# Transposes of a constant in TensorE's expected gaps, and up weights requested at the top of a step, in a hybrid mixer and feed-forward layer

## The chip, the cores and the metric

The kernel runs on one core of a Trainium2 chip. The metric is the device time of one execution in microseconds (us). The engines are TensorE (PE, with its weight loads PEld), VectorE (DVE), ScalarE (ACT), GpSimd (POOL) and SyncE (SP), which issues every DMA in this kernel.

## The reference

One layer over a sequence of 2048 tokens of width 1024, float32 throughout:

```python
def reference(x, norm1_w, w_in, ...):
    for l in range(DEPTH):                       # DEPTH = 1
        h = rms_norm(x, norm1_w[l])
        proj = h @ w_in[l]                       # 1024 -> 3344 columns
        (g_q, g_k, g_v, g_z, g_b, g_a, m_q, m_k, m_v, m_o, m_i, m_f, s_u) = jnp.split(proj, split_idx, axis=-1)
        y_a = gated_deltanet(g_q, g_k, g_v, g_z, g_b, g_a, ...)   # 4 heads of 128, conv of 4 taps, chunked delta rule
        y_b = mlstm(m_q, m_k, m_v, m_o, m_i, m_f, ...)            # 4 heads of 64, chunked
        y_c = s5_mixer(s_u, ...)                                  # 16 groups of 16 channels, 64 complex states
        y = jnp.concatenate([y_a, y_b, y_c], axis=-1)
        x = x + y @ w_out[l]
        x = x + conv_ffn(rms_norm(x, norm2_w[l]), w_up[l], ffn_conv_w[l], ffn_conv_b[l], w_down[l])
    return rms_norm(x, final_norm_w)

def conv_ffn(x, w_up, conv_w, conv_b, w_down):   # D_FF = 2816
    h = causal_depthwise_conv(x @ w_up, conv_w) + conv_b          # 3 taps
    gate, up = jnp.split(h, 2, axis=-1)
    return (jax.nn.silu(gate) * up) @ w_down
```

## The kernel before

Large products are done as three matmuls of a type fp32r: each operand is split into a rounded high part (an ACT copy) and a low part (a subtraction, mostly on POOL), and high x high, high x low and low x high are summed in PSUM (`split`, `mm`).

*Mixing stage (`main_a`).* The sequence is cut in 4 blocks of 512 tokens. For each block some 26 projections of 128 columns (`proj`, 24 matmuls of 512 columns each) run in an order written out in `ORDER`. Each is followed by `follow`, which drains its PSUM bank and starts the convolution, and when a head's value projection is through, a generator `gdn` for that head. `gdn` computes the chunked delta rule of one head and one block: transposes, Gram products, an inverse in six levels, and then a chain over 4 chunks in which three matmuls alternate with DVE and ACT reads of the same PSUM tile `sq0` or `sq1` (by the parity of n = 4 x block + head; three quarters of the tile are used). `mlstm`, `gates` and the `s5_` functions are further generators. The last two projections of a block run interleaved in `last_two`, while the next block's normed input is transposed. `w_split` splits the projection weights ahead; `w_two` lowers the number it may keep ready.

*Who goes next.* The whole program is laid out by a planner at build time; each engine executes its own instructions in exactly that order, and waits at run time only on semaphores. `Engine` wraps an engine: each call is first entered into a `Clock`, then emitted. `Clock.note` computes when the instruction could start (the engine free, its inputs written, PSUM readers taking turns, outputs free) and how long it takes by fixed costs: a transpose of n columns 2n/2400 us (0.107 us for 128), an fp32r matmul n/2400 + 0.0025. A PSUM tile counts as one piece there. The loop `drive` asks the running generators in turn, and steps the one whose needs are met earliest by that clock. When nothing is ready the clock moves on: there it expects TensorE to stand.

*Output product.* `out_proj` multiplies the mixed output by `w_out`; when the mixers are through, `ffn_pools` closes the PSUM pool of the mixing stage and opens that of the feed-forward stage.

*Feed-forward stage (`ffn`).* Two halves of 1024 tokens. For each, 22 pairs of an up product by `up_pair`, which multiplies the 2 x 2 blocks with 7 products instead of 8 (operand sums of the weights made by POOL in `sum12` and `make`), then two down products of 512 tokens (`down`), whose result is normed and stored by `final`. Weights come through a ring: `raw_load` issues a DMA of 512 KB into one of NRAW = 4 raw tiles `f_wr`; `make` takes the next item of `todo` (kinds U, M, D), splits it into parts `f_ph`, `f_pl` (NPART = 8), and marks raw tiles free in `freed`. The next call of `make` issues the loads for these. `make` is called after every product (`up_pair`) or block of products (`down`). It returns at once when the ring has no free slot, or when the next item is of kind U and the up stage's pool `fu` is not open:

```python
        if not self.todo or self.ring < (1 if self.todo[0][0] == "U" else 2):
            return
        G = self.G
        kind, j = self.todo[0]
        if kind == "U" and self.fu is None:
            return

        while self.freed:
            self.freed -= 1
            self.raw_load()
```

Names in the profile: psq, psz, psx and the like are PSUM banks of projections and transposes, sd_ names those of `gdn`, sq its chain, psf the up and psd the down product, f_S the sums of raw weights, d_x and d_h, d_l the down product's moving blocks. Nearly all instructions have the line of the wrapper `call` (L169).

Of the kernel before, what the change touches and what calls it, by code (L numbers as in the profile page):

```python
# [7 lines left out]
F32 = mybir.dt.float32  # L8
# [9 lines left out]
P = 128  # L18
# [5 lines left out]
NCB = BT // P  # L24
# [22 lines left out]
class Clock:  # L47
# [5 lines left out]
    def __init__(self):  # L53
        self.free = {e: 0.0 for e in ("T", "V", "A", "G", "S", "dge", "dma")}
        self.wr, self.rd, self.table, self.slots = {}, {}, None, {}
        self.cold = 0.0
# [46 lines left out]
                t = max(t, end + own.get(by, other))  # L103
        return t

    def note(self, e, op, args, kw):
        out = kw.get("out", args[0] if args else None)
        outs = [self.span(a) for a in (out, kw.get("accum_out")) if a is not None]
        ins = [v for k, v in kw.items() if k not in ("out", "accum_out") and hasattr(v, "tensor")]

        turns = [self.span(v) for v in ins if v.space == PSUM]
        ins = [self.span(v) for v in ins]
        t = self.free[e]
        for a in ins:
            t = max(t, self.after(self.wr, a, {e: self.DRAIN[e]}, self.SEM))
        for a in turns:
            t = max(t, self.after(self.rd, a, {e: -1.0}, self.SEM))
        for a in outs:
            for log in (self.wr, self.rd):
                t = max(t, self.after(log, a, {e: -1.0}, self.SEM))  # L120
        if e == "S":
            self.free["S"] = t + 0.05
            self.free["dge"] = max(self.free["dge"], t) + 0.46
            n = out.shape[0] * self.size(out) * 4
            self.free["dma"] = max(self.free["dma"], self.free["dge"]) + n / 360e3
            end = self.free["dma"] + 1.6
        else:
            c = self.cost(e, op, out, kw)
            if e == "T":
                c += min(c, max(0.0, self.cold - t))  # L130
            end = self.free[e] = t + c
        for name, rs in ins:
            d = self.rd.setdefault(name, {})
            if end > d.get(rs, (0.0, e))[0]:
                d[rs] = (end, e)
        for name, rs in outs:
            for log in (self.wr, self.rd):
                d = log.setdefault(name, {})
                for k in [k for k in d if all(any(lo <= a and b <= hi for lo, hi in rs) for a, b in k)]:
                    del d[k]  # L140
            self.wr[name][rs] = (end, e)
# [18 lines left out]
class Engine:  # L160
    def __init__(self, clock, key, eng):
        self.clock, self.key, self.eng = clock, key, eng

    def __getattr__(self, op):
        f = getattr(self.eng, op)

        def call(*args, **kw):
            self.clock.note(self.key, op, args, kw)
            return f(*args, **kw)  # L169
        return call  # L170
# [18 lines left out]
class Hybrid:  # L189
# [32 lines left out]
    def exp(self, y, x, n, r, q, i):  # L222
# [9 lines left out]
        V.tensor_scalar(out=i, in0=n, scalar1=127.0, scalar2=8388608.0, op0=ALU.add, op1=ALU.mult)  # L232
        V.scalar_tensor_tensor(out=y, in0=q, scalar=1.0, in1=i.bitcast(F32), op0=ALU.add, op1=ALU.mult)


    def setup(self):
        nc, ins, V, A, S = self.nc, self.ins, self.V, self.A, self.S
        cp = self.const = self.pool("const")
        self.dram = self.pool("dram", space=DRAM)
        self.pctx = ExitStack()  # L240
        self.ps = self.pool("ps", space=PSUM, ctx=self.pctx)
        self.ident = cp.tile([P, P], F32, name="ident")
        S.dma_start(out=self.ident, in_=self.cst_d[C_ID])

# [258 lines left out]
    def last_two(self, b, n, ops, take, follow):  # L503

        pr = []
        self.kdone = 0
        for j, (kind, i) in enumerate(ops):
            w, ps = yield from take(kind, i, n + j)
            pr.append((kind, i, ps, self.proj(ps, *w)))
            self.w_two = j  # L510
            if j == 0:
                self.add_side(self.norm_next(b + 1, n + 2), True)
        for k in range(KD):
            for p in pr:
                yield next(p[3])
            self.kdone = k + 1
        self.w_two = 0
        for kind, i, ps, g in pr:
            for _ in g:
                pass  # L520
            follow(kind, i, ps)
# [106 lines left out]
    def main_a(self):  # L628
        self.posts = self.posted = self.drained = self.hblock = n = 0
        for b in range(NB):  # L630
            st = {"tiles": [[] for _ in range(H)], "z": [[] for _ in range(H)]}

            def take(kind, i, n):
                if kind == "q":
                    yield lambda: len(self.gdn_live) < 4
                if kind in "qz":
                    yield lambda: self.y_done > b * H + i - (Q_BUFS if kind == "q" else Z_BUFS)
                if kind == "mq" and i == 0:
                    yield lambda: not self.ml_busy
                    self.ml_busy = True  # L640
                    for nm in ("mk", "mv", "mo"):
                        st[nm] = self.mp.tile([P, 2, BT], F32, tag=nm, name=nm)
                yield lambda: self.w_rdy
                w = self.w_rdy.pop(0)
                if n == 0:
                    yield lambda: self.xdone >= b
                    yield tuple(self.xq)
                if b and kind == "g":
                    yield lambda: len(self.hN[1]) > 4
                tag = f"b{n % 3}"  # L650
                yield w[1], tag, lambda: self.drained >= n - 2
                return w, self.ps.tile([P, BT], F32, tag=tag, bufs=1, name="ps" + kind)

            def follow(kind, i, ps):
                self.add_side(self.post(self.follow(b, kind, i, ps, st)))
                if kind == "v":
                    self.gdn_live.append(Side(self.gdn(b, i, st["tiles"][i], st["z"][i], st)))

            ops = [op[:2] for op in self.ops_a(b)]
            last = ops[-2:] if b < NB - 1 else []  # L660
            for kind, i in ops[:len(ops) - len(last)]:
                w, ps = yield from take(kind, i, n)
                if kind == "g":
                    yield from self.norm1(n, ps, w) if b == 0 else self.proj_next(ps, *w)
                else:
                    yield from self.proj(ps, *w)
                n += 1
                follow(kind, i, ps)
            if last:
                yield from self.last_two(b, n, last, take, follow)  # L670
                n += 2
# [94 lines left out]
    def gdn(self, b, h, tiles, gz, gt):  # L766
        V, A, G, T, S = self.V, self.A, self.G, self.T, self.S
        n = b * H + h
# [3 lines left out]
        sh = [P, NCB, P]  # L772
# [34 lines left out]
        kdec = big("kdec", 3)  # L807
# [18 lines left out]
        rs, t = sm("rs", 2 * NCB), sm("t", 2 * NCB)  # L826
        self.rsqrt(rs, ssq, t)
        rk, rq = rs[:, 0:NCB], rs[:, NCB:2 * NCB]
        c1, b2, nc2 = sm("c1"), sm("b2"), sm("nc2")
# [26 lines left out]
        vb = c3(vT)  # L856
# [10 lines left out]
        for lev in range(1, NM):  # L867
# [6 lines left out]
            for c in range(NCB):  # L874
# [4 lines left out]
                            op=ALU.mult)  # L879
# [23 lines left out]
        self.inv_done += 1  # L903
        yield Vi

        tag = f"sq{n % 2}"
        yield lambda: self.seq_done[n % 2] == n // 2
        states = [self.Sst[h]]
        yield vb, kdec, states[0], tag
        p = self.ps.tile(sh, F32, tag=tag, bufs=1, name=tag)  # L910
        for c in range(NCB):
            T.matmul(out=p[:, 0, :], lhsT=cs(kT, c), rhs=states[c], start=True, stop=True)
            V.scalar_tensor_tensor(out=vb[:, c, :], in0=p[:, 0, :], scalar=nc2[:, c:c + 1], in1=vb[:, c, :],
# [554 lines left out]
    def ffn_pools(self):  # L1468

        self.wctx.close()  # L1470
        self.lctx.close()
        self.pctx.close()
        self.ps = self.pool("ps2", space=PSUM)
        self.bufs = {"big": 5, "sd": 3, "y": 1, "yh": 2, "yl": 2}
        self.bq = self.operands(self.pool("kp", ctx=self.rctx), 5)
        self.fw = self.pool("fw", ctx=self.rctx)
        self.op = self.pool("op", ctx=self.octx)
        self.ffn_plan()
        self.add_side(self.first_build())
# [209 lines left out]

    def make(self):  # L1690

        if not self.todo or self.ring < (1 if self.todo[0][0] == "U" else 2):
            return
        G = self.G
        kind, j = self.todo[0]
        if kind == "U" and self.fu is None:
            return

        while self.freed:
            self.freed -= 1  # L1700
            self.raw_load()
        self.todo.pop(0)
        if kind != "U":
            w = self.raws.pop(0)
# [315 lines left out]

    def run(self):
        self.now = 0.0
        self.bufs = {"b0": 1, "b1": 1, "b2": 1, "sd": 3, "sq0": 1, "sq1": 1, "e_X": 1, "acc": 3, "wh": 3, "wl": 3,
                     "y": 1, "yh": 2, "yl": 2}
        self.misc, self.gdn_live, self.ml_live = [], [], []
        self.inv_done = self.e_done = self.y_done = 0
# [89 lines left out]
```

## Time and profile before

| | |
|---|---|
| time, median of 3 runs | 2985.22 us (2973.05 to 2985.95) |
| time of the profiled execution | 2976.19 us |
| its span, first to last instruction | 2974.2 us |
| busy, share of the span | PE 91%, PEld 75%, DVE 71%, ACT 44%, POOL 45% |
| mean granted TensorE clock | 0.958 of full speed |
| DMA | 312.69 MB, 105 GB/s over the span |

The page's second part cuts the span in 40 slices of 74 us; each digit is the busy share in tenths, and PEclk is the clock that the throttle granted to TensorE. The mixing stage with the output product takes about the first half of the span, feed-forward the second. In a row of the timeline, the time in brackets is the engine's idle time before the instruction, and after the arrow stands what ended it. A matmul's duration is from its start to its modelled end; the time it takes of the engine is from its start to the next one's start.

### The profile page before, as it was taken

To read this page: it belongs to the slowest core of one execution; us is meant where nothing else is said; L and a number is where in the kernel's file an instruction comes from. 1 tells how busy PE (TensorE), PEld (TensorE's weight loads), DVE (VectorE), ACT (ScalarE), POOL (GpSimd) and SP (SyncE) were. 2 spreads that over 40 slices of the span, in tenths; PEclk is the share of its full clock that TensorE was granted. 3 is DMA by queue.
4 is the path that set the end of the run, shared out by engine and by line. 5 is a ranking of instruction groups with operands and counts; after the bars stand their busy time and mean duration, and the time that the engine had idled before them with its cause. 6 is when DMAs were issued, how large, how long until landed. Compare 5 with 4: busy or idle time off the path is not lost.

```text
span 2974.2 us, 38960 instructions
## 1 busy us (share of the span) xinstructions
PE 2708.9 (91%) x13298; PEld 2234.2 (75%) x13298; DVE 2114.7 (71%) x4346; ACT 1294.9 (44%) x2798; POOL 1325.8 (45%) x960
## 2 busy tenths in 40 slices
PE   6797788988998989889998999999998999999997
PEld 5686677877887778577776888877786888887876
DVE  6876668678765886663558888887546998895364
ACT  4544344444544354632335444445333554543232
POOL 3361122223322243221137888862225998883221
PEclk9898789989999999989999999999999999999999
DMA  4223212133222324335653222235552222224452
GB/s 123 77 84 95 79 46 80 54 90 99 63 59 61 93 77 113 91 97 184 213 175 102 78 86 81 76 107 191 187 181 71 85 86 85 76 81 138 163 177 103
DMA packets 364380, 312.69 MB, mean 105 GB/s; under 512 B 41043, under 2 KB 299222, under 8 KB 364182
## 3 DMA queue, kind: packets, MB, share of 16 engines
q1 hardware_dynamic: 364182, 310.21, 33.4%
q8 instruction: 105, 1.72, 0.2%
q14 instruction: 93, 0.76, 0.1%
HBM read 245.01 MB, written 65.14 MB: 104 GB/s over the span
## 4 chain that ended last, share of the span: by engine, by line
PE 49%; DVE 4%; issue 3%; POOL 1%; ACT 1%; DMA 1%; SPq 0%; DVEq 0%; ACTq 0%; POOLq 0%
PE psf L169 28%; PE psd L169 14%; PE pso L169 4%; POOL f_pl L169 1%; DMA x_d<-o_x 1%; DVE acc L169 0%; PE psx L169 0%; PE sd_pw L169 0%; DVE bl L169 0%; POOL f_S L169 0%; DVE d_l L169 0%; PE pz L169 0%; PE sd_p L169 0%; DVE d_ss L169 0%; PE sq L169 0%
## 5 line engine op out<-in xcount | busy, mean ns | idle before, releaser
L169 POOL TENSOR_TENSOR f_pl<-f_wr,f_ph 128x512 fp32r<-128x512 f32 x274 | 407.5, 1490 | 455.8 <-ACT f_ph L169 425.1
L169 POOL TENSOR_TENSOR wl<-wr,wh 128x1024 fp32r<-128x1024 f32 x108 | 258.5, 2396 | 582.3 <-ACT wh L169 518.9
L169 PE MATMUL psf<-bh,f_pl 128*128 128x512 f32 x1232 | 491.5, 399 | 10.8 <-POOL f_pl L169 10.8
L169 PE MATMUL psf<-bh,f_ph 128*128 128x512 f32 x1232 | 491.7, 399 | 6.3 <-ACT f_ph L169 4.2
L169 PE MATMUL psf<-bl,f_ph 128*128 128x512 f32 x1232 | 491.5, 399 | 1.4 <-DVE bl L169 1.3
L169 DVE SCALAR_TENSOR_TENSOR f_cv<-f_rw,fpar,f_cv 128x512 f32<-128x512 f32 x352 | 480.2, 1384 | 17.5 <-ACT f_rw L169 11.3
L169 ACT ACTIVATE f_ph<-f_wr 128x512 fp32r<-128x512 f32 x360 | 212.4, 619 | 233.9 <-issue 177.0
L169 PEld LDWEIGHTS psf<-bh,f_pl 128*128 128x128 f32 x1232 | 233.8, 190 | 68.9 <-POOL f_pl L169 12.1
L169 PEld LDWEIGHTS psf<-bh,f_ph 128*128 128x128 f32 x1232 | 233.8, 190 | 64.4 <-ACT f_ph L169 5.0
L169 PEld LDWEIGHTS psf<-bl,f_ph 128*128 128x128 f32 x1232 | 233.7, 190 | 60.0 <-DVE bl L169 3.1
L169 ACT ACTIVATE f_cv<-f_rw,fpar 128x512 f32<-128x512 f32 x176 | 142.9, 812 | 307.5 <-DVE f_rw L169 305.1
L169 PE MATMUL psd<-f_ph,d_h 128*128 128x512 f32 x640 | 253.8, 397 | 9.2 <-ACT f_ph L169 8.1
L169 PE MATMUL psd<-f_pl,d_h 128*128 128x512 f32 x640 | 252.7, 395 | 4.9 <-DVE f_pl L169 3.8
L169 PE MATMUL psd<-f_ph,d_l 128*128 128x512 f32 x640 | 252.3, 394 | 1.1 <-DVE d_l L169 1.1
L169 POOL TENSOR_TENSOR f_pl<-f_S,f_ph 128x512 fp32r<-128x512 f32 x132 | 218.7, 1659 | 8.3 <-ACT f_ph L169 4.4
L169 DVE TENSOR_TENSOR f_pl<-f_wr,f_ph 128x512 fp32r<-128x512 f32 x86 | 84.3, 989 | 174.7 <-ACT f_ph L169 174.7
L169 PEld LDWEIGHTS psd<-f_ph,d_h 128*128 128x128 f32 x640 | 121.4, 190 | 36.6 <-ACT f_ph L169 8.7
L169 PEld LDWEIGHTS psd<-f_pl,d_h 128*128 128x128 f32 x640 | 121.4, 190 | 32.9 <-DVE f_pl L169 4.6
L169 PEld LDWEIGHTS psd<-f_ph,d_l 128*128 128x128 f32 x640 | 121.4, 190 | 29.9 <-DVE d_l L169 2.8
L169 ACT ACTIVATE wh<-wr 128x1024 fp32r<-128x1024 f32 x108 | 114.1, 1056 | 39.8 <-PE psz L169 20.8
L169 ACT ACT_TABLE_LOAD x83 | 106.5, 1283 | 31.8 <-DVE acc L169 29.6
L169 POOL TENSOR_TENSOR yl<-y,yh 128x1024 fp32r<-128x1024 f32 x16 | 39.3, 2456 | 167.6 <-ACT yh L169 167.6
(524 smaller groups left out, 6343.7 us busy)
## 6 DMA issues: line engine op xcount, KB each, us to landing
wr<-in_w_in_dram SPq DMA_DIRECT2D x104, 512.0 KB
f_wr<-in_w_up_dram SPq DMA_DIRECT2D x88, 512.0 KB
f_wr<-in_w_down_dram SPq DMA_DIRECT2D x88, 512.0 KB
mid_d<-f_cv SPq DMA_DIRECT2D x88, 256.0 KB
d_x<-mid_d SPq DMA_DIRECT2D x80, 256.0 KB
xt<-in_x_dram SPq DMA_DIRECT2D x16, 512.0 KB
y<-y_d SPq DMA_DIRECT2D x16, 512.0 KB
d_a<-x_d SPq DMA_DIRECT2D x32, 256.0 KB
```

The lines of the kernel that those rows point to most:

```text
L169: return f(*args, **kw)
```

## The change

`Engine` gets a hook `idle`. On TensorE it is set to the new function `spin` from the first `follow` of the mixing stage until `ffn_pools`. Before each TensorE instruction, the wrapper asks the planner's clock when it could start and hands the difference to TensorE's free time to `spin`. If that is over 0.5 us, `spin` emits as many transposes of the 128 x 128 identity as fill 60% of the difference by the planner's cost. They write into the fourth quarter of `sq1`'s bank, which nothing reads. For this, `sq0` and `sq1` become two tiles that are allocated once; a head no longer asks for a tag. In `last_two`, `w_two` is set before the projection's weights are taken, not after. In `make`, the loads for freed raw tiles are issued before the tests for a free slot and an open pool.

```diff
-    def note(self, e, op, args, kw):
+    def begin(self, e, op, args, kw):
...
+        return t, out, outs, ins
+
+    def note(self, e, op, args, kw):
+        t, out, outs, ins = self.begin(e, op, args, kw)
...
 class Engine:
     def __init__(self, clock, key, eng):
         self.clock, self.key, self.eng = clock, key, eng
+        self.idle = None
...
         def call(*args, **kw):
+            if self.idle:
+                self.idle(self.clock.begin(self.key, op, args, kw)[0] - self.clock.free[self.key])
             self.clock.note(self.key, op, args, kw)
...
+    def spin(self, gap):
+
+        if gap > 0.5:
+            self.T.idle = None
+            for _ in range(int(0.6 * gap * 2400 / (2 * P))):
+                self.T.transpose(out=self.spill, in_=self.ident, identity=self.ident)
+            self.T.idle = self.spin
...
+        self.sq = [self.ps.tile([P, NCB, P], F32, name=f"sq{i}") for i in range(2)]
+        self.spill = self.sq[1][:, 3, :]
...
         for j, (kind, i) in enumerate(ops):
+            self.w_two = j
             w, ps = yield from take(kind, i, n + j)
             pr.append((kind, i, ps, self.proj(ps, *w)))
-            self.w_two = j
...
             def follow(kind, i, ps):
+                self.T.idle = self.spin
...
-        tag = f"sq{n % 2}"
         yield lambda: self.seq_done[n % 2] == n // 2
         states = [self.Sst[h]]
-        yield vb, kdec, states[0], tag
-        p = self.ps.tile(sh, F32, tag=tag, bufs=1, name=tag)
+        yield vb, kdec, states[0]
+        p = self.sq[n % 2]
...
         self.lctx.close()
+        self.T.idle = None
         self.pctx.close()
...
     def make(self):
 
+
+        while self.freed:
+            self.freed -= 1
+            self.raw_load()
         if not self.todo or self.ring < (1 if self.todo[0][0] == "U" else 2):
             return
...
-
-        while self.freed:
-            self.freed -= 1
-            self.raw_load()
         self.todo.pop(0)
```

More of the change, by code (lines that the diff above doesn't have):

```diff
@@ L2022, in run @@
         self.now = 0.0
-        self.bufs = {"b0": 1, "b1": 1, "b2": 1, "sd": 3, "sq0": 1, "sq1": 1, "e_X": 1, "acc": 3, "wh": 3, "wl": 3,
+        self.bufs = {"b0": 1, "b1": 1, "b2": 1, "sd": 3, "e_X": 1, "acc": 3, "wh": 3, "wl": 3,
                      "y": 1, "yh": 2, "yl": 2}
```

## The prediction

> **What bounds the kernel now.** I read the page first, for engine shares and the granted clock in 40 slices, then the busy times of chosen stretches, the waits of TensorE and the timeline around its longest stalls.
>
> ```profile
> PE 2708.9 (91%) x13298; PEld 2234.2 (75%) x13298; DVE 2114.7 (71%) x4346; ACT 1294.9 (44%) x2798; POOL 1325.8 (45%) x960
> PE   6797788988998989889998999999998999999997
> PEclk9898789989999999989999999999999999999999
> ```
>
> The same by stretch (columns: length, busy time and count of each engine, granted clock, DMA share, GB/s). The first row is the mixing stage in which the transposes can be emitted, the second the feed-forward stage.
>
> ```profile
> core 0: us, PE busy (x) PEld busy (x) DVE busy (x) ACT busy (x) POOL busy (x), PEclk, DMA share, GB/s
> 29.00:1345.00 1316.00, 1140.61 (x6553) 972.99 (x6552) 935.61 (x2749) 593.09 (x1306) 391.52 (x356) 0.93 0.28 82
> 1600.00:2976.00 1376.00, 1321.34 (x5622) 1063.26 (x5620) 1023.24 (x1213) 589.41 (x1276) 840.95 (x548) 0.98 0.34 113
> 100.00:150.00 50.00, 34.95 (x170) 28.54 (x169) 41.46 (x122) 27.97 (x68) 14.39 (x10) 0.83 0.29 84
> 250.00:300.00 50.00, 32.08 (x190) 28.54 (x189) 22.68 (x78) 25.18 (x63) 7.13 (x3) 0.84 0.33 106
> 300.00:350.00 50.00, 39.12 (x196) 32.82 (x196) 27.23 (x96) 16.37 (x45) 7.30 (x4) 0.79 0.23 74
> 1250.00:1300.00 50.00, 39.32 (x203) 31.02 (x203) 34.86 (x76) 23.79 (x46) 12.79 (x6) 0.80 0.37 118
> ```
>
> Feed-forward is TensorE end to end (1321 of 1376 us). The mixing stage has 1316 - 1141 = 175 us of TensorE idle time and a mean clock of 0.93. The clock is not a smooth quantity; in steps of 3.41 us it is 1.00 or 0.50:
>
> ```profile
> 239.20:242.61 3.41, 1.50 (x14) 1.31 (x15) 3.27 (x12) 0.37 (x1) 0.39 (x1) 1.00 0.54 153
> 242.61:246.02 3.41, 3.41 (x13) 3.02 (x13) 3.20 (x19) 0.64 (x2) 0.00 (x0) 0.50 0.00 1
> 949.15:952.56 3.41, 0.42 (x2) 0.00 (x1) 0.00 (x0) 3.13 (x4) 2.04 (x1) 1.00 0.00 0
> 952.56:959.39 6.83, 4.55 (x21) 4.55 (x22) 3.74 (x9) 5.28 (x8) 0.30 (x1) 0.50 0.38 115
> 962.81:966.22 3.41, 1.97 (x12) 1.25 (x12) 2.79 (x8) 1.68 (x4) 1.64 (x1) 1.00 0.17 41
> 966.23:969.64 3.41, 0.95 (x5) 0.71 (x6) 1.70 (x3) 3.31 (x13) 0.00 (x0) 1.00 0.65 191
> 969.64:973.05 3.41, 3.41 (x12) 2.75 (x12) 2.67 (x7) 0.64 (x3) 0.00 (x0) 0.50 0.00 0
> ```
>
> A step with little work (1.50, 0.42, 0.95 us busy) is followed by one at half speed, in which TensorE has its backlog to do (3.41 of 3.41 busy); a step with 1.97 us busy is followed by full speed. Half-clock time in the mixing stage is 2 x 0.07 x 1316 = 184 us. In the four slices above, rich in it, TensorE is busy 145.5 of 200 us, 73%; so about 134 us of its work runs at half speed, and 67 us of TensorE time is the most that a warm clock returns.
>
> **Change 1: the transposes.** Where the planner's clock expects one TensorE instruction to start more than 0.5 us after TensorE is free, 60% of that gap is filled with transposes of the identity. Do transposes hold the clock, and what does one cost?
>
> ```profile
> 17.34 2.18 PE L169 MATMUL psx<-ident,xt 128*128 128x128 f32 x9 [2.34 <-DVE sg L169]
> 19.17 0.78 PE L169 MATMUL psg<-hh,wh 128*128 128x512 f32 x1
> ...
> 22.96 0.60 PE L169 MATMUL psx<-ident,xt 128*128 128x128 f32 x4
> 23.32 0.48 PE L169 MATMUL psg<-hh,wh 128*128 128x512 f32 x1
> ...
> 963.22 1.97 PE L169 MATMUL psx<-ident,xt 128*128 128x128 f32 x12 [1.77 <-DVE hl L169]
> ```
>
> From start to next start, four took 0.36 us at full clock (0.09 each) and nine took 1.83 us at half clock (0.20 each); the planner books 0.107. The step 962.81 to 966.22 held these twelve transposes and nothing else, 1.97 us, and the next step is still at 1.00: they count. The Trainium skill, "TensorE: Matmul & The Clock Gate", Part 4 (PE-mode transpose), speaks against the change: it says that full speed does not engage for transposes, which do not count as busy in the same way. The row above disagrees.
>
> Gain. Sixty per cent of even an empty step is 2.05 us, above the 1.97 that held the clock; the step at 949.15 would come to 0.42 + 0.6 x 2.99 = 2.21. So a stall that the planner foresees keeps the clock, and what is not foreseen loses it as now. I take 60% foreseen: 40 of the 67 us. What a faster TensorE hands on to the end is bounded by none (the other engines' chain sets the pace) and all. The waits name DVE and ACT:
>
> ```profile
> PE sd_v L169 <- DVE g_D L169: 10.1, 6, 3.9
> PE psx L169 <- DVE hl L169: 10.0, 5, 3.4
> PE sq L169 <- DVE g_kdec L169: 8.3, 6, 3.5
> ```
>
> but DVE is busy only 936 of 1316 us there, TensorE 1141, so I take half: -20 us, ends 0 and -67. Late next is DVE, the releaser of most of these waits.
>
> Cost. If the planner saw exactly the 175 us of idle time, 105 us of transposes (some 1000) would go in, all into time that is empty: 0. If none of it were really empty, TensorE would have 105 us more work. The planner is static and counts no half clock, so some is wrongly placed: I take a fifth, 21 us, half of it handed on, +10 (ends 0 and +105). In a gap that begins at half clock a transpose takes 0.20 us instead of the booked 0.107, and the filling overruns the gap by a fifth; that is in the same term.
>
> The target is the fourth quarter of the second state-chain tile. The planner books a PSUM tile as a whole, so for it a transpose waits for the last DVE or ACT reader of that tile. Whether the program's semaphores do so too, no row shows. If so, before a chain matmul of an odd head the filling starts only when the gap ends:
>
> ```profile
>   PE sq L169: 19.1, 13
> L169 DVE SCALAR_TENSOR_TENSOR gv<-sq,s_nc,gv x64: 335/344/352, 202.0 to 1359.3; 128x128 f32<-128x128 f32 x64
> ```
>
> TensorE idled 19.1 us before those matmuls, half of it in odd heads, 60% of that is 5.7 us; elsewhere a reader is 0.34 us long. From 0 to +6, I take +2.
>
> **Change 2: raw weights requested first in a step.** Of the up stage nothing changes as long as a step finds a free slot. It changes at the passage from the first half's down product to the second half's up product, where a step returned before its load because the up pool was not open yet:
>
> ```profile
> 2221.95 9.24 SPq L169 DMA_DIRECT2D f_wr<-in_w_up_dram  x3
> 2267.72 9.73 SPq L169 DMA_DIRECT2D out_dram<-d_a  x8
> 2277.55 19.93 SPq L169 DMA_DIRECT2D f_wr<-in_w_up_dram  x5
> ...
> 2264.17 1.29 POOL L169 TENSOR_TENSOR f_pl<-f_S,f_ph 128x512 fp32r<-128x512 f32 x1
> 2282.72 1.26 POOL L169 TENSOR_TENSOR f_S<-f_wr 128x512 f32<-128x512 f32 x1 [17.26 <-DMA f_wr<-in_w_up_dram]
> ...
> 2276.64 0.40 PE L169 MATMUL psf<-bl,f_ph 128*128 128x512 f32 x1
> 2286.60 0.79 PE L169 MATMUL psf<-bh,f_pl 128*128 128x512 f32 x1 [9.56 <-POOL f_pl L169]
> 2287.00:2291.00 4.00, 4.00 (x11) 3.08 (x11) 1.16 (x2) 3.12 (x9) 4.00 (x4) 0.55 0.00 0
> 2289.80 6.13 DVE L169 SCALAR_TENSOR_TENSOR f_cv<-f_rw,fpar,f_cv 128x512 f32<-128x512 f32 x4 [8.93 <-ACT f_rw L169]
> ```
>
> Four raw tiles exist. Three up weights are requested by 2231, the fourth only at 2277.55, behind eight output stores; it lands at 2282.72, and POOL, 17.26 us idle, then forms its sum. TensorE stands 9.56 us and works the next 4 us at half clock. With the load at the top of the next step, the fourth request follows the third at about 2231 to 2233, SP being free until 2267.72; by the 5.2 us from request to landing above it is there before 2240. POOL goes on at 2265.5, and after two sums and a split (1.26 us each) the part is ready near 2269.3, 7 us before TensorE needs it. What is late next: DVE, 8.93 us idle in that stall behind the same ACT queue, moves forward with it, so no new wait is due. Gain 9.6 + 2 (half of 4 us) = -11.5 us; the ends are 0 (another wait there) and -12.
>
> Every other early load is one step earlier on the in-order SP queue. At the two passages from up to down it gets ahead of the fourth block of products:
>
> ```profile
> 2007.73 5.58 SPq L169 DMA_DIRECT2D d_x<-mid_d  x4
> ```
>
> Those four took 5.58 us, so one more ahead of them costs at most a quarter of that, 1.4 us, at each of two passages. The buffer it asks for was split a step before, and the products that it delays are needed after the three already under way: I take 0, ends -3 and +3.
>
> **Change 3: the earlier count in the last two projections** delays one weight split at three block ends until the last projection has its weights. Cover: the two projections' own 48 matmuls. If that cover is gone, ACT and POOL times from the page are the price:
>
> ```profile
> L169 ACT ACTIVATE wh<-wr 128x1024 fp32r<-128x1024 f32 x108 | 114.1, 1056 | 39.8 <-PE psz L169 20.8
> L169 POOL TENSOR_TENSOR wl<-wr,wh 128x1024 fp32r<-128x1024 f32 x108 | 258.5, 2396 | 582.3 <-ACT wh L169 518.9
> ```
>
> 3 x (1.06 + 2.40) = 10 us at most; its load is queued behind it on SP, as now. I take 0. The state tiles, allocated once instead of per head, cost nothing: the same heads take turns on them. That the planner may order the mixing stage differently has no row; I bound it by that 10 us, both ways.
>
> **The sum**, against the profiled execution of 2976.19 us (span 2974.2 and 2.0 around it): -20 + 10 + 2 - 11.5 = -19.5, about 2957 us. The runs' median is 2985.22, 9 us above that execution, their lowest 2973.05; a change under 0.5% (15 us) can't be told from none.
>
> **The rivals.**
> *Most of the clock comes back.* If the planner's stalls are TensorE's, nothing is misplaced, 90% of 67 us returns and 0.6 of it is handed on: -36 - 11.5, about 2928. For it: the long waits are few and on named chains. Against: DVE at 71%.
> *Wrong places (slower).* The planner's gaps are not TensorE's: transposes stand in front of matmuls whose operands are there. With a misplaced share m, cost 52 m + 2, clock gain 25 (1 - m), load gain 11.5: break-even at m = 0.45; at 0.7 it is +20, 2996 us. For it: a static schedule that knows neither half clock nor longer operations. Against: the waits are on the longest chains, which any plan should see.
> *The filling is neutral*, or the early load meets another wait while the filling gains a little: between -11.5 and 0, about 2967.
> *Transposes don't hold the clock.* Then only costs remain: +10 + 2 - 11.5, about 2977. This is what the change would do by the page named above; the twelve transposes speak against it.
>
> **How the numbers follow.** Forecast (2940 to 2970) 0.40, clock back 0.18, neutral 0.18, no hold 0.07, wrong places 0.17. Faster by over 0.5%: 0.18, 0.36 of the forecast's 0.40, and 0.02 of neutral, 0.56. Slower: most of wrong places, 0.15, and 0.01 of no hold. The rest, 0.28, is within. The range 2918 to 2992 leaves out the extreme half of the first rival and most of the slower one, some 2 in 10 together.
>
> **What would show it.** Right: several hundred more 128x128 identity matmuls in the mixing stage, its clock near 0.97, its length about 10 us less; no DMA wait before f_S at the second half's start, and psf there without a wait over 2 us. Wrong: the clock still 0.93 (not foreseen, or no hold); TensorE busy time up with DVE's waits on TensorE longer (wrong places); the transposes' first wait on a DVE or ACT reader of the state tile; the down-to-up passage with another releaser.

## The result and the profile after

The changed kernel takes 3014.31 us (median, 3012.59 to 3015.89) against 2983.27 us before in the same comparison: ratio 1.011, interval 1.0085 to 1.0136. It is slower by 31 us, where 2957 us and a gain had been forecast. The rows below are from the two profiled executions, which lie 37 us apart (2976.19 and 3013.28 us).

The page after: busy shares, slices, clock, and the row of the new transposes (the last figures are idle time before them and what ended it).

```profile
PE 2782.8 (92%) x14014; PEld 2314.9 (77%) x14014; DVE 2116.2 (70%) x4359; ACT 1287.6 (43%) x2792; POOL 1326.9 (44%) x960
PE   7897998897999899978998999998998999999997
PEclk9998989999999999979999999999999999999999
L177 PE MATMUL sq<-ident 128*128 128x128 f32 x716 | 107.0, 312 | 22.0 <-DVE gv L177 11.4
```

The stretch from 29 us to the first up product, first before, then after (length, busy times, clock, DMA share, GB/s). But for the transposes, the work in it is nearly the same in both:

```profile
29.00:1547.20 1518.20, 1326.17 (x7427) 1124.00 (x7425) 1039.62 (x3043) 660.25 (x1435) 426.95 (x371) 0.94 0.33 96
29.00:1588.20 1559.20, 1398.67 (x8142) 1204.17 (x8140) 1035.69 (x3056) 652.85 (x1429) 424.18 (x372) 0.95 0.32 93
```

All of the loss lies here: the stretch is 41 us longer, and the rest 4 us shorter. The 716 transposes are there, the clock is a little better, but 107 us of transposes took the place of only 192 - 160.5 = 31.5 us of idle time. And the transposes wait: 22 us in all, for DVE and ACT operations that read the chain tile in whose bank they write. One such place, first TensorE's rows and then DVE's:

```profile
528.44 0.39 PE L177 MATMUL sq<-S,gk 128*128 128x128 f32 x2
532.49 4.16 PE L177 MATMUL sq<-ident 128*128 128x128 f32 x21 [3.66 <-DVE gv L177]
536.48 0.60 PE L177 MATMUL sd_py<-ident,gq 128*128 128x128 f32 x4
...
530.70 0.69 DVE L177 TENSOR_TENSOR gq<-sd_o,s_ro 128x512 f32<-128x512 f32 x1
531.31 0.52 DVE L177 TENSOR_TENSOR e_x<-e_rot 128x144 f32<-128x144 f32 x2
531.86 0.31 DVE L177 TENSOR_TENSOR e_Cr<-e_x,e_x 128x144 f32<-128x144 f32 x1
532.09 0.34 DVE L177 SCALAR_TENSOR_TENSOR gv<-sq,s_nc,gv 128x128 f32<-128x128 f32 x1
```

The gap is there, 3.66 us, and it stays empty. The 21 transposes meant for it wait for DVE's read of another quarter of their bank. That read takes only 0.34 us, but DVE does other operations first, and it is over at 532.43. Then the transposes take 4 us of their own in front of sd_py, whose operand gq was written by 531.39. The matmuls behind them here, those of sd_py, are not matmuls of the chain.

At the passage to the second half's up product the fourth load is early (four requests from 2263.14 on), and POOL waits for no DMA, but TensorE now waits for DVE:

```profile
2263.14 12.94 SPq L177 DMA_DIRECT2D f_wr<-in_w_up_dram  x4
2319.16 10.76 SPq L177 DMA_DIRECT2D out_dram<-d_a  x8
...
PE psf L177 <- DVE f_u L177: 5.7, 1, 5.7
```

### The profile page after: what moved, and what is told of

Its sections match the earlier page's. It is cut to its first block, busy times and chain, and to the rows that moved or that the text cites. A ratio compares the mean times of both kernels' runs of the same rounds, so it can differ in the third digit from the quotient of the medians.

```text
span 3011.5 us, 40452 instructions
## 1 busy us (share of the span) xinstructions
PE 2782.8 (92%) x14014; PEld 2314.9 (77%) x14014; DVE 2116.2 (70%) x4359; ACT 1287.6 (43%) x2792; POOL 1326.9 (44%) x960
## 5 line engine op out<-in xcount | busy, mean ns | idle before, releaser
L177 DVE TENSOR_TENSOR f_pl<-f_wr,f_ph 128x512 fp32r<-128x512 f32 x86 | 93.7, 1098 | 178.4 <-ACT f_ph L177 178.4
L177 PE MATMUL sq<-ident 128*128 128x128 f32 x716 | 107.0, 312 | 22.0 <-DVE gv L177 11.4
L177 PEld LDWEIGHTS sq<-ident 128*128 128x128 f32 x716 | 100.4, 166 | 26.1 <-DVE gv L177 12.0
```

## The experiments

Two theories for the mixing stage. 1: the transposes that are executed cost the time, by waiting for readers of the bank (1a) or by standing in the wrong places (1b). 2: booking them turns the planner's order, and the order costs the time. Ratios are to the kernel before, run beside. Its own median went from 2978.81 to 2983.27 us between the comparisons, so a difference between runs of two comparisons is given by the medians and, in brackets, by the ratios.

**The early load alone** (`raw_only`): of the diff only the change in `make`.

> The kernel before with the early load alone; no transposes, the planner's order of all engines as before, only SP's order differs. Theory A (the early load works as the changed kernel's trace shows: POOL no longer waits for the DMA, but DVE's small norm operations take 1.2 us instead of 0.16 us each while POOL works, and TensorE then waits for DVE): the second half's up stage loses 4 to 5 us against the kernel before, ratio 0.9985, with one wait of psf for DVE f_u of 5 to 6 us. Rival (the prediction's step): 11.5 us, ratio 0.996, no psf wait over 2 us there.

2976.74 us, ratio 0.9993 (0.9981 to 1.0006), not distinguishable from before by its time. Its trace is the one that theory A expects: from the first product of the second up stage to the first of the down stage it takes 443.3 us (before 447.1). Waits of TensorE, DVE's operations and the last of POOL's series at that place:

```profile
PE psf L169 <- DVE f_u L169: 5.3, 1, 5.3
...
2256.61 0.16 DVE L169 SCALAR_TENSOR_TENSOR d_ss<-d_ss,d_rs 128x1 f32<-128x1 f32 x1
2256.80 1.20 DVE L169 SCALAR_TENSOR_TENSOR d_rs<-d_ss,d_rs 128x1 f32<-128x1 f32 x1
...
2281.18 0.16 DVE L169 SCALAR_TENSOR_TENSOR d_ss<-d_ss,d_rs 128x1 f32<-128x1 f32 x1
...
2278.01 1.75 POOL L169 TENSOR_TENSOR f_pl<-f_wr,f_ph 128x512 fp32r<-128x512 f32 x1
```

DVE's operations on one column take 1.20 us from 2256.80, where POOL's series of operations has begun, and 0.16 us again at 2281.18, after POOL's series ends at 2279.8. In the whole trace, the 176 operations on d_ss and d_rs that ran with POOL idle took at most 0.16 us each; the 32 that overlapped a POOL operation had a median of 1.20 us. With the load early, POOL works without a pause here, and so DVE is slow for as long.

**Order and filling apart.** `booked_only` has the changed kernel's order on every engine without its transposes; `fill_old_order` has the order of before (and the early load), with 591 transposes.

```diff
 # booked_only, against the changed kernel
-                self.T.transpose(out=self.spill, in_=self.ident, identity=self.ident)
+                self.clock.note("T", "transpose", (), dict(out=self.spill, in_=self.ident, identity=self.ident))
 # fill_old_order: emitted past the clock; w_two set after take, as before
+                self.nc.tensor.transpose(out=self.spill, in_=self.ident, identity=self.ident)
```

> The changed kernel with its transposes entered into the planner's clock but not emitted: every engine has the changed kernel's order, without the 716 transposes. Theory 1 (the transposes that are executed cost the time): about 30 us under the changed kernel, ratio to the kernel before 0.996 to 1.001. Theory 2 (the planner's other order costs the time, the transposes are neutral): within 6 us of the changed kernel, ratio 1.009 to 1.011.

> The early load, and 591 transposes emitted without being entered into the clock, so that all other instructions stand in the order of the kernel before (the count in the last two projections as before too). Theory 1 (transposes cost): 20 to 30 us slower than the early load alone, ratio to the kernel before 1.006 to 1.009. Theory 2 (order costs): not slower than the early load alone, ratio 0.993 to 0.999, mean clock at 0.97.

`booked_only`: 3008.91 us, 1.0104 (1.0086 to 1.0121): as theory 2 says, the order alone costs 32 us against the early load alone. `fill_old_order`: 2996.26 us, 1.0052 (1.0035 to 1.0068): theory 1 holds as well, the transposes alone cost 19.5 us. The stretch up to the first up product, for the early load alone, the order alone and the filling alone:

```profile
29.00:1551.90 1522.90, 1332.08 (x7426) 1129.20 (x7424) 1039.16 (x3043) 660.22 (x1435) 426.81 (x371) 0.93 0.33 96
29.00:1582.30 1553.30, 1360.07 (x7427) 1156.53 (x7425) 1037.26 (x3056) 652.96 (x1429) 424.02 (x371) 0.92 0.32 94
29.00:1568.80 1539.80, 1379.92 (x8017) 1181.65 (x8015) 1042.09 (x3043) 659.88 (x1435) 426.44 (x372) 0.95 0.33 95
```

In the second row, TensorE's idle time is that of the first (193 and 191 us); the loss is in its busy time, which is 28 us longer, at a lower clock. By the clock records of the two traces, TensorE is busy at half clock for 150.5 us in the first and 208.6 us in the second. Half of the 58 us between them is 29 us, so the order's loss is lost clock.

**The earlier count** (`w_two_only`): the early load, and `w_two` set before `take`.

> The kernel before with the early load and the earlier count in the last two projections; no transposes, nothing booked. It parts the 32 us that the changed order cost. Theory 2a (the order goes wrong because the planner books each run of transposes behind the DVE or ACT reader of a PSUM tile as a whole, and counts TensorE as stalled until then): this kernel is as fast as the early load alone, ratio 0.997 to 1.002. Theory 2b (the earlier count, which holds back a weight split at block ends, does it): as slow as the kernel with booked transposes, 1.008 to 1.012.

2976.83 us, 0.9993 (0.998 to 1.0006): no cost. So the 32 us come from the booking. When only the time of the transposes is booked and not their wait for readers, the plan as built has exactly the order of `w_two_only` on every engine: what turns the order is the booked wait. The two state tiles that are allocated once are not in this run; `fill_old_bank` and `mended_no_fill` below have them, at 1.0006 and 0.9989, so they show no cost either.

**Another bank.** In `other_bank` (changed order) and `fill_old_bank` (old order) each run of transposes is emitted to the fourth quarter of that chain tile whose readers are expected to be done first:

```diff
+            to = min(self.sq, key=lambda t: self.clock.after(self.clock.rd, self.clock.span(t), {"T": -1.0}, 0.0))
...
+                self.nc.tensor.transpose(out=to[:, 3, :], in_=self.ident, identity=self.ident)
```

> The changed kernel, same order, same 716 transposes, each run of them written into that one of the two chain tiles whose DVE and ACT readers the planner expects to be done first (20 of 52 runs go to the other tile). Theory 1a (in the changed kernel transposes wait for a reader of the bank, 22 us of idle time before them in its trace, and then stand before ready work): those 22 us and some 18 us of late filling mostly go, 10 to 25 us under the changed kernel, ratio 1.002 to 1.007. Theory 1b (they are simply in the wrong places) and theory 2: within 6 us of the changed kernel, 1.009 to 1.013.

> The 591 transposes in the old order, each run into the chain tile whose readers the planner expects to be done first (30 of 49 runs to the other tile). If waiting for a reader of the bank is a main part of the 19.5 us that the filling costs in the old order (20.1 us of idle time stands before its runs), 8 to 15 us of these go: ratio 1.000 to 1.003. If the places are wrong whatever the bank: within 5 us of the old filling, 1.004 to 1.007.

`other_bank`: 3006.01 us, 1.0088 (1.0065 to 1.0111), 8 us (7) under the changed kernel, with intervals that overlap. `fill_old_bank`: 2978.17 us, 1.0006 (0.9996 to 1.0016), 18 us (14) under the filling in the old bank, at the upper end of what was expected or above it. With most of the wait gone, no cost of the filling is left that can be told from none. The transposes in the old bank and in the right one:

```profile
L248 PE MATMUL sq<-ident 128*128 128x128 f32 x591 | 80.8, 292 | 20.1 <-DVE gv L177 10.7 <-ACT gv L177 7.1 <-DVE g_kdec L177 1.6
...
L249 PE MATMUL sq<-ident 128*128 128x128 f32 x591 | 81.7, 294 | 6.9 <-ACT gv L177 6.9
```

**How much is filled** (`fill_old_bank_03` and `_09`: factor 0.3 and 0.9 for 0.6; `fill_long`: only gaps over 2 us).

> The same with 30% of each gap filled instead of 60%. If overfilling is the cost (75 us of transposes took the place of 31 us of idle time only), half the transposes cost less than half and the clock still gains something: 0.996 to 1.001, mean clock 0.960 to 0.965, perhaps faster than the early load alone. If the cost goes with the number of runs and not with their length: 1.002 to 1.005.

> Old order, the right bank, 90% of each gap filled (899 transposes). With 30% and 60% the time was that of the early load alone within 4 us, though TensorE's half-clock time fell from 212 to 157 and 126 us. Theory 3 (the warm clock's gain and the transposes that stand before ready work cancel, and the second grows with the filling): 8 to 20 us slower than the early load alone, ratio 1.002 to 1.006. Rival (TensorE's time is not what the stage waits for, whatever is done to it): still within 4 us, 0.999 to 1.001.

> Old order, the right bank, 60%, but only gaps that the planner expects to last over 2 us: 478 of the 591 transposes in 24 of the 49 runs. If the short gaps are where the planner errs and the long ones where the clock is lost: 3 to 8 us under the filling of all gaps, ratio 0.997 to 0.999. If the cost lies in the long runs of transposes: no change, 1.000 to 1.002.

30%: 2980.24 us, 1.0005 (0.9992 to 1.0018). 90%: 2991.88 us, 1.0025 (1.0011 to 1.0039), 15 us (10) over the early load alone, as theory 3 says; from the 60% it is 14 us (6) away, with intervals that just overlap. Long gaps only: 2981.63 us, 1.0012 (0.9999 to 1.0024): leaving out the short gaps gained nothing. For 60% and 90%:

```profile
29.00:1555.60 1526.60, 1375.04 (x8019) 1178.42 (x8017) 1047.73 (x3043) 659.58 (x1435) 427.49 (x371) 0.96 0.33 96
29.00:1569.20 1540.20, 1404.62 (x8325) 1210.69 (x8324) 1045.76 (x3043) 660.18 (x1435) 426.82 (x371) 0.96 0.33 95
```

The clock is no better at 90% (0.96), and TensorE's other work at half clock is the same (88 and 87 us by the clock records), so the extra transposes are only in the way.

**The changed kernel, mended** (`mended`: the choice of `to` above, also for the booking), its order without transposes (`mended_no_fill`), and with the transposes put back into the second tile's bank (`mended_old_bank`).

> The changed kernel with one thing mended: each run of transposes goes, on the chip and in the planner's booking, to the chain tile whose readers are expected to be done first. By the planner's own clock the mixing stage then ends at 1148 us, against 1130 in the order of before, 1138 with the earlier count and 1165 in the changed kernel. Theory 2a (booking behind a reader makes the bad order, waiting for it on the chip makes the filling dear): most of the 31 us goes, ratio 1.000 to 1.005. Rival (any booking of transposes turns the order, which differs from that of before from the same place on): 1.007 to 1.011.

> The mended kernel's order on every engine, its 713 transposes booked but not emitted. If the filling's warm clock pays in this order: 5 to 20 us slower than the mended kernel, ratio 0.999 to 1.004. If the filling is neutral as in the old order: within 4 us of it, 0.996 to 0.9985.

> The mended kernel's order, its transposes written to the second chain tile only, as in the changed kernel, whatever its readers do. If the wait for the readers costs on the chip what it cost in the old order (18 us) or in the changed order (8 us): 8 to 20 us slower than the mended kernel, ratio 1.000 to 1.004. If all of the loss was the planner's order: within 4 us of the mended kernel.

`mended`: 2971.33 us, 0.9972 (0.9955 to 0.9988): the loss is gone, and more than theory 2a expected. `mended_no_fill`: 2976.75 us, 0.9989 (0.9973 to 1.0004). `mended_old_bank`: 3000.85 us, 1.0062 (1.0039 to 1.0086). In that order:

```profile
29.00:1544.30 1515.30, 1383.24 (x8138) 1192.72 (x8136) 1026.01 (x3056) 654.86 (x1431) 423.87 (x371) 0.96 0.33 96
29.00:1549.40 1520.40, 1344.10 (x7427) 1145.77 (x7425) 1026.70 (x3056) 654.39 (x1431) 424.76 (x372) 0.93 0.33 96
29.00:1576.20 1547.20, 1398.82 (x8140) 1207.75 (x8138) 1031.32 (x3056) 654.53 (x1431) 424.84 (x371) 0.95 0.33 94
...
L177 PE MATMUL sq<-ident 128*128 128x128 f32 x713 | 100.9, 299 | 4.2 <-ACT gv L177 4.2
...
L250 PE MATMUL sq<-ident 128*128 128x128 f32 x713 | 108.9, 315 | 22.2 <-DVE gv L177 12.8 <-ACT gv L177 7.0 <-DVE g_kdec L177 2.4
```

In one and the same order, the bank alone is worth 29.5 us (27), more than expected. In the right bank the account is: 101 us of transposes, 44 us less idle time, and 1344 - (1383 - 101) = 62 us less of TensorE's other work: -5 us. The 62 us are not all the clock's. 16 us of the transposes' time overlaps other matmuls in the records; taken alone, the other matmuls are busy 1344 and 1298 us, 46 us less. Of that time, 174 and 76 us are at half clock, and half of the difference is 49 us, so the 46 us fit the clock's return. Whether the -5 us are a gain can't be told: the intervals of `mended` and `mended_no_fill` overlap.

**The batched norm.** In `raw_batched`, `final` for the first half's second 512 tokens is done once for all four tiles (13 small DVE operations instead of 52); `two_batched` is that with the earlier count, `mended_batched` that with the mended filling.

```diff
+            self.inv_rms(rs[:, 0, :], ss, rs[:, 1, :])
+            for t in range(NT):
+                for c in range(2):
...
-                        if c:
+                        if c and (blk != 1 or t == NT - 1):
                             self.add_side(final(t))
```

> The early load alone, and the norm of the first half's last 512 outputs done in one set of 13 small DVE operations instead of four sets. Theory A (DVE's small operations, 1.2 us each beside POOL's work, make DVE late for the up products, and TensorE waits 5.3 us for it): that wait goes and the second up stage takes 437 to 440 us instead of 443, 4 to 8 us under the early load alone, ratio 0.995 to 0.998. Rival (the wait has another cause): no change against the early load alone.

> The earlier count, the early load and the batched norm, no transposes: each was no loss alone. If they add up, ratio 0.9955 to 0.998, the fastest here, with no psf wait over 1 us at the second half's start. If the batched norm's gain was chance: 0.999 to 1.001.

> The mended kernel with the batched norm. If the two add up, 4 to 9 us under the mended kernel, ratio 0.994 to 0.9965; if not, 0.996 to 0.998.

`raw_batched`: 2972.30 us, 0.9975 (0.9963 to 0.9987); its second up stage takes 434.9 us, and of the wait for DVE there is left:

```profile
PE psf L169 <- DVE f_u L169: 0.7, 1, 0.7
```

`two_batched`: 2974.46 us, 0.998 (0.9965 to 0.9995), not the fastest as expected but not to be told from `raw_batched`. `mended_batched`: 2967.64 us, 0.9957 (0.9941 to 0.9972), the fastest by its median, though its interval overlaps that of `mended`: 12 us under the kernel before, 47 us (46) under the changed one.

## Why the prediction was wrong

*The steps that failed* are two terms, both about the bank to which the transposes are written.

The first is the planner's order. The prediction said that another order "has no row", took it at 0 and bounded it by 10 us, from a row that has to do with weight splits; the bound had no ground. In place of 0 the runs showed 32 us (33) (`w_two_only` to `booked_only`), as much as the whole loss of the changed kernel. What turns the order is the planner's booking of the transposes behind the readers of the bank. The prediction named this booking, but not what it does to the order.

The second is the term for the bank on the chip, "From 0 to +6, I take +2". It priced only chain matmuls of odd heads, by their own idle time of 19.1 us, and elsewhere the length of a reader, 0.34 us. In its place the runs showed that the transposes wait 22 us for readers, before any instruction whose gap is filled. What counts is when the reader is through and not how long it runs: DVE came to the read shown above only after other operations. The filling then follows after the gap: 18 us (14) in the old order (`fill_old_order` to `fill_old_bank`), 29.5 us (27) in the mended one. The two costs do not add up: with the changed order the filling adds 5 us (2), and the bank is worth 8 (7), neither clear of none.

Two of the signs of being wrong that the prediction named came true: the transposes' first wait is for a DVE reader of the state tile, and the passage from down to up has another releaser.

*Cost of the filling by its place.* +10 was predicted, and -20 for the clock, together -10. Measured in the right bank: +1 (+4) in the old order, -5 in the mended one, neither distinguishable from 0. The mechanism is as described. The clock returned 46 us in the mended order, near the 40 us that were assumed of the 67. But of 85 us that the transposes add to TensorE's busy time, 44 came out of idle time. So the share in the wrong place was up to a half (41 us), not a fifth, and that eats the clock's gain. It is an upper bound, as a faster TensorE also opens new idle time. The overrun of a gap that begins at half clock is by the prediction's own numbers an eighth (0.6 x 0.20 / 0.107 = 1.12), not a fifth. The rival "wrong places", with break-even at 0.45, was the right warning; the changed kernel's loss of 31 us has its sign, but not its mechanism.

*Transposes hold the clock*: right. The order of `mended` runs at a mean clock of 0.953 without them and 0.971 with them, and its half-clock time up to the first up product falls from 225 to 120 us. So the rule in "TensorE: Matmul & The Clock Gate", Part 4, of the Trainium skill does not hold for these float32 transposes.

*The early load*, -11.5: POOL's wait for the load went as forecast, but the gain was 4 us (2), and not clear of none by time. The step that failed is "no new wait is due": DVE was late next, with its small operations at 1.2 us. With these cut to a quarter, the up stage is 12 us shorter than before (447.1 to 434.9 us); some 5 us of it are given back ahead of it, where the first up product starts later.

*The earlier count and the state tiles*, 0: right for the count (0.9993); for the tiles no run has them alone, and those that have them in the old or the mended order show no cost.

What stays open: which of the moved steps makes the booked order lose the clock. The rows show that the loss is busy time at a lower clock and not idle time; no run moved single steps.

## What to carry to other kernels

Work that is to fill a gap must not wait for the engines that the gap waits for: here an unread quarter of a bank was tied to the readers of the others. Price a dependency of new instructions for every place where they will stand, by when it is met and not by how long its last operation runs. Where a planner books them, look at the plan's own end first. By its clock the mixing stage went from 1130 to 1165 us, a plan's figure and no measurement, but with the right sign. It is an alarm and no forecast: it says 1138 us for `w_two_only` and 1148 for the mended order, and neither was measured slower. Filler that holds a clock is paid in engine time: it is worth at most what the clock returns, and here up to half of it did not come out of idle time.

## What the runs showed of the hardware

DVE operations on a 128 x 1 tile took 0.16 us alone and 1.20 us while POOL worked on 128 x 512 tiles; doing them once for four tiles, 13 instead of 52, took TensorE's wait for DVE from 5.3 to 0.7 us.

Float32 transposes of a 128 x 128 tile held TensorE's clock: 713 of them in an unchanged order took its half-clock time up to the first up product from 225 to 120 us (`mended_no_fill` and `mended`).
